# A row softmax gradient on one core: loads split by row over two queues, and some blocks stored whole

## The chip, the cores and the metric

The kernel runs on 1 core of one Trainium2 chip. The metric is device time in microseconds (us), the median of several runs. Besides the compute engines (TensorE or PE, VectorE or DVE, ScalarE or ACT, GpSimd or Pool, and SyncE or SP, which computes nothing), the core has 16 DMA engines. A DMA is issued by an instruction on one of the engines' queues (here SP, ACT or Pool); the 16 DMA engines then carry it out.

## The reference

It is the gradient of a cross-entropy loss with respect to the logits: the softmax of every row minus the one-hot label.

```python
batch, seq_len, vocab = 8, 1024, 8192       # logits float32, labels integers
logits_max = np.max(logits, axis=-1, keepdims=True)
exp_logits = np.exp(logits - logits_max)
softmax = exp_logits / np.sum(exp_logits, axis=-1, keepdims=True)
one_hot[batch_idx, seq_idx, labels] = 1.0
return (softmax - one_hot).astype(np.float32)
```

There are 8192 rows of 8192 float32 values: 268.4 MB are read and 268.4 MB are written.

## The kernel before, in words

The rows are cut into 32 blocks of 256. In a block, partition p of 128 holds rows 2p and 2p+1, which lie next to each other in memory. "Row" from here on means one such half of a block: 128 partitions times one row of 8192 values, 4 MB. There are 64 of them, numbered t = 2b + j for block b and j = 0 (even) or 1 (odd). The tile `X` has three slots (`SLOTS`) of one block each, so block b uses the slot that block b-3 used, and everything is computed in place.

For each row t the work is:

- DVE takes the row's negated maximum `m` (`row_max`), which waits for the row's load.
- ACT computes the exponential in place, with its sum `s`.
- DVE takes the reciprocal `r` of that sum.
- ACT multiplies the row by `r`.
- DVE subtracts the one-hot label: it compares `iota` (column numbers, kept in PSUM) with the label and subtracts (one `scalar_tensor_tensor`).
- ACT issues the row's store.

The order on each engine is written out by hand in the loop over t. On DVE, the maximum of row t+1 stands before the subtraction of row t. On ACT, the store of row t-1 stands between the exponential and the scaling of row t. The last row's scaling and subtraction are done in two halves.

How a block is moved is set by one letter for each block in `LOADS` and `STORES`. With `r` it goes as two transfers, one for each row: every partition moves a contiguous run of 32 KB in each. With `w` it goes as one transfer: every partition moves one run of 64 KB. (A third letter, `h`, is not used.) In `store`, a whole block goes out when its odd row is finished, since a piece is stored with the last row that it holds.

`load(b)` issues all loads on SP. Each load waits for those stores of block b-3 that meet its piece. The helper `run` (line 63) issues every instruction, gives it its waits and has it count up a semaphore. That is why nearly all lines of the profile carry L68, the line in `run` where the instruction is made. `got` are the semaphores that loads count up, `put` those of the stores, one set for each slot.

Before the change, blocks 0 to 4 and 26 to 31 are loaded by row, blocks 5 to 25 whole, and every block is stored by row.

Of the kernel before, what the change touches and what calls it, by code (L numbers as in the profile page):

```python
# [8 lines left out]
G = 2  # L9
SLOTS = 3  # L10


LOADS = "rrrrrwwwwwwwwwwwwwwwwwwwwwrrrrrr"
STORES = "rrrrrrrrrrrrrrrrrrrrrrrrrrrrrrrr"


@with_exitstack
def kernel(
# [6 lines left out]
    nc = tc.nc  # L25
# [29 lines left out]

    with tc.tile_critical():  # L56
        sem = tc.alloc_semaphore
        got = [[sem(f"got{i}{q}") for q in range(2)] for i in range(SLOTS)]
        put = [[sem(f"put{i}{q}") for q in range(2)] for i in range(SLOTS)]
        lab_got, dve, act, pe, pool = (sem(n) for n in ("lab_got", "dve", "act", "pe", "pool"))  # L60
        count = {}
# [1 line left out]
        def run(engine, waits, counter, method, **operands):  # L63

            waits = list(dict.fromkeys(waits))
            for w in waits[:-1]:
                engine.wait_ge(*w)
            instruction = getattr(engine, method)(**operands)  # L68
            for w in waits[-1:]:
                instruction._wait_ge(*w)  # L70
            step = 16 if method == "dma_start" else 1
            instruction.then_inc(counter, step)
            count[counter.name] = count.get(counter.name, 0) + step
            return counter, count[counter.name]
# [36 lines left out]
        def meets(a, b):  # L111

            sets = [[set(range(*d.indices(n))) for d, n in zip(p, (P, G))] for p in (a, b)]
            return all(x & y for x, y in zip(*sets))
# [5 lines left out]
        def load(b):  # L120
            loaded[b] = []
            before = stored.get(b - SLOTS, last_made if b == SLOTS - 1 else [])
            for q, piece in enumerate(PIECES[LOADS[b]]):
                ps, js = piece
                free = [w for other, w in before if meets(piece, other)]
                w = run(
                    nc.sync, free, got[b % SLOTS][q], "dma_start",
                    out=X[ps, b % SLOTS, js, :], in_=x_b[b, ps, js, :],
                )
                loaded[b].append((piece, w))  # L130

        def store(t):
            b, j = divmod(t, G)
            stored.setdefault(b, [])
            for q, piece in enumerate(PIECES[STORES[b]]):
                ps, js = piece
# [19 lines left out]


        load(0)
        w_max = row_max(0)
        for t in range(T):  # L160
# [7 lines left out]
            if t + 1 < T:  # L168
                if (t + 1) % G == 0:
                    load((t + 1) // G)  # L170
                w_max = row_max(t + 1)
# [53 lines left out]
```

## Time and profile before

| What | us |
|---|---|
| Median of 3 runs | 1248.09 |
| Lowest and highest run | 1247.96, 1249.02 |
| Span of the profiled execution | 1245.7 |
| DVE busy | 1119.2 |
| ACT busy | 919.1 |
| Pool busy | 7.4 |
| DVE: one row's maximum, mean | 8.68 |
| DVE: one row's subtraction, mean | 8.61 |
| ACT: one row's exponential, mean | 7.12 |
| ACT: one row's scaling, mean | 7.02 |

The span is the time from the first to the last instruction of the one execution that was profiled; no other time of that execution is on record, and the median of the timed runs is 2.4 us above its span. The page also lists, for each DMA queue, its packets, the megabytes and the time that its packets took as a share of 16 engines' span. A packet is one contiguous run that one DMA engine moves. Queue q1 is that of SP, q10 that of ACT.

### The profile page before, as it was taken

Reading aid. Unit: us, or ns where it says so; the run is one execution under the profiler, and the core shown is the slowest. Engines: PE = TensorE matmul, PEld = TensorE weight load, DVE = VectorE, ACT = ScalarE, POOL = GpSimd, SP = SyncE. Lnnn points to the kernel's source line nnn. Section 1 sums busy time; section 2 is a strip of 40 time slices with the busy share of each in tenths; the row PEclk is TensorE's granted clock in tenths of the full one; section 3 lists DMA queues with packets and bytes.
Section 4 is the critical chain, followed back from the end, with each engine's and each line's share of the span. In section 5 each row is a group of like instructions: output and inputs, shape, how many; then the busy total and the mean of one; then the engine's idle time right before and its main releaser. Section 6 shows DMA issues by size and latency. Waiting matters only on the chain.

```text
span 1245.7 us, 592 instructions
## 1 busy us (share of the span) xinstructions
PE 0.4 (0%) x2; PEld 0.3 (0%) x2; DVE 1119.2 (90%) x196; ACT 919.1 (74%) x194; POOL 7.4 (1%) x7
## 2 busy tenths in 40 slices
PE   0000000000000000000000000000000000000000
PEld 0000000000000000000000000000000000000000
DVE  5999998888988889888998888988889999999893
ACT  3888886778776787767877778777777788887772
POOL 2000000000000000000000000000000000000000
DMA  9999999999999999999999999999999999999998
GB/s 406 417 429 433 438 433 442 437 426 427 430 435 445 439 417 442 426 430 437 432 443 438 420 435 432 430 437 450 420 426 437 436 428 432 437 435 429 432 437 386
DMA packets 15460, 536.98 MB, mean 431 GB/s; under 512 B 1728, under 2 KB 1728, under 8 KB 1760
## 3 DMA queue, kind: packets, MB, share of 16 engines
q1 hardware_dynamic: 6192, 268.44, 50.0%
q10 hardware_dynamic: 9264, 268.51, 49.9%
q14 instruction: 4, 0.03, 0.0%
HBM read 268.50 MB, written 268.44 MB: 431 GB/s over the span
## 4 chain that ended last, share of the span: by engine, by line
DMA 59%; DVE 37%; another core or an unknown queue 2%; ACT 1%; DVEq 0%; issue 0%; PE 0%; SPq 0%; ACTq 0%
DMA X<-in_logits_dram 31%; DMA out_dram<-X 27%; DVE m L68 18%; DVE X L68 18%; ACT X L68 1%; DVE iota L68 0%; DVEq L56 0%; DMA lab_raw<-in_labels_dram 0%; DVE lab_f L68 0%; DVE r L68 0%; PE iota L68 0%; SPq L68 0%; ACTq L68 0%; DVE lab L68 0%
## 5 line engine op out<-in xcount | busy, mean ns | idle before, releaser
L68 DVE TENSOR_REDUCE m<-X 128x1 f32<-128x8192 f32 x64 | 555.2, 8675 | 94.3 <-DMA X<-in_logits_dram 94.3
L68 ACT ACTIVATE X<-X,m 128x8192 f32<-128x8192 f32 x64 | 455.9, 7123 | 188.4 <-DVE m L68 188.4
L68 DVE SCALAR_TENSOR_TENSOR X<-iota,lab,X 128x8192 f32<-128x8192 int16 (+1 forms) x65 | 559.7, 8612 | 4.1 <-ACT X L68 4.1
L68 ACT ACTIVATE X<-X,r 128x8192 f32<-128x8192 f32 (+1 forms) x65 | 456.0, 7017 | 115.9 <-DVE r L68 115.9
L68 DVE RECIPROCAL r<-s 128x1 f32<-128x1 f32 x64 | 9.9, 154 | 7.3 <-ACT X L68 7.3
L68 ACT ACTIVATION_READ_ACCUMULATOR X<-X,m 128x1 f32 x64 | 12.0, 187 | 0.0
L68 DVE CAST lab_f<-lab_raw 32x256 f32<-32x256 int32 x1 | 3.7, 3685 | 4.7 <-DMA lab_raw<-in_labels_dram 4.7
L68 POOL IOTA X<- 128x8192 int16 x1 | 6.9, 6944 | 0.0
L68 DVE TENSOR_SCALAR iota<-X 128x4096 int32<-128x4096 int32 x1 | 4.4, 4427 | 0.1
L68 ACT ACT_TABLE_LOAD x1 | 1.3, 1283 | 1.3 <-SPq L56 1.3
L68 DVE COPY lab<-iota 128x64 f32<-128x64 f32 x1 | 0.2, 225 | 0.5 <-PE iota L68 0.5
L68 PE MATMUL iota<-ident,lab_f 32*128 32x32 f32 x2 | 0.4, 300 | 8.5 <-DVE lab_f L68 8.5
L68 PEld LDWEIGHTS iota<-ident,lab_f 32*128 32x128 f32 x2 | 0.3, 196 | 8.4 <-DVE lab_f L68 8.4
L68 POOL TENSOR_SCALAR_AFFINE_SELECT ident<-ident 32x32 f32<-32x32 f32 x1 | 0.2, 204 | 0.1
L68 POOL MEMSET ident<- 32x32 f32 x1 | 0.1, 115 | 0.5 <-SPq L56 0.5
L209 POOL MEMSET const-bfloat16-1.0<- 128x1 bf16 x1 | 0.1, 107 | 0.0
L209 POOL MEMSET const-uint8-127<- 128x1 uint8 x1 | 0.1, 107 | 0.0
L209 POOL MEMSET const-float32-0.0<- 128x1 f32 x1 | 0.1, 104 | 0.2 <-issue 0.2
L209 POOL MEMSET const-float32-1.0<- 128x1 f32 x1 | 0.1, 104 | 0.0
## 6 DMA issues: line engine op xcount, KB each, us to landing
out_dram<-X ACTq DMA_DIRECT2D x64, 4096.0 KB, 30.8
X<-in_logits_dram SPq DMA_DIRECT2D x22, 4096.0 KB, 26.6
X<-in_logits_dram SPq DMA_DIRECT2D x21, 33.4
lab_raw<-in_labels_dram ACTq DMA_DIRECT2D x1, 64.0 KB, 3.8
```

What stands on the lines that cost most here:

```text
L68: instruction = getattr(engine, method)(**operands)
L209: nc = _bacc.Bacc("TRN2", target_bir_lowering=False, num_devices=1)
```

## The change

Three things change. All blocks are now loaded by row. From block 3 on (`SOLO`, the fourth block), the odd row of a block is issued on Pool's queue instead of SP's; even rows, and all of blocks 0 to 2, stay on SP. Blocks 6, 10, 14, 18 and 22 are stored whole, all others by row as before.

```diff
-LOADS = "rrrrrwwwwwwwwwwwwwwwwwwwwwrrrrrr"
-STORES = "rrrrrrrrrrrrrrrrrrrrrrrrrrrrrrrr"
+LOADS = "rrrrrrrrrrrrrrrrrrrrrrrrrrrrrrrr"
+SOLO = 3
+STORES = "rrrrrrwrrrwrrrwrrrwrrrwrrrrrrrrr"
...
-        got = [[sem(f"got{i}{q}") for q in range(2)] for i in range(SLOTS)]
+        got = [[sem(f"got{i}{q}") for q in range(G + 1)] for i in range(SLOTS)]
...
             for q, piece in enumerate(PIECES[LOADS[b]]):
                 ps, js = piece
                 free = [w for other, w in before if meets(piece, other)]
+                queue = nc.gpsimd if b >= SOLO and q else nc.sync
                 w = run(
-                    nc.sync, free, got[b % SLOTS][q], "dma_start",
+                    queue, free, got[b % SLOTS][G if queue is nc.gpsimd else q], "dma_start",
                     out=X[ps, b % SLOTS, js, :], in_=x_b[b, ps, js, :],
                 )
```

The loads become 64 transfers of one row, 35 on SP and 29 on Pool. The stores become 54 transfers of one row and 5 of a whole block, all on ACT. The work of DVE, ACT and PE and its order stay as they were. A load of a block whose slot was last stored whole (blocks 9, 13, 17, 21 and 25) waits, for both its rows, for that one store.

## The prediction

> **What bounds the kernel now.** I read the page first, for the engines and the DMA queues. PE and Pool are as good as unused. VectorE (DVE) is busy for 90% of the span, but the 16 DMA engines have work in 9 tenths or more of every slice but the last.
>
> ```profile
> span 1245.7 us, 592 instructions
> PE 0.4 (0%) x2; PEld 0.3 (0%) x2; DVE 1119.2 (90%) x196; ACT 919.1 (74%) x194; POOL 7.4 (1%) x7
> DMA  9999999999999999999999999999999999999998
> ...
> q1 hardware_dynamic: 6192, 268.44, 50.0%
> q10 hardware_dynamic: 9264, 268.51, 49.9%
> ...
> out_dram<-X ACTq DMA_DIRECT2D x64, 4096.0 KB, 30.8
> X<-in_logits_dram SPq DMA_DIRECT2D x22, 4096.0 KB, 26.6
> X<-in_logits_dram SPq DMA_DIRECT2D x21, 33.4
> ```
>
> Queue q1 is SP's (loads), q10 is ScalarE's (ACT, stores); together they fill 99.9% of 16 engines. That 43 loads left 6192 packets and 64 stores 9216 (plus 48 for the labels) tells how a transfer is cut: 144 packets each, which are 128 pieces, one for each partition, and 16 completions of 4 bytes. So a row transfer moves 32 KB pieces and a whole-block transfer 64 KB pieces, eight on each engine.
>
> Next come the windows, to see whether the share holds in every stage. The last two columns are the DMA share and GB/s.
>
> ```profile
> 47.00:160.00 113.00, 0.00 (x0) 0.00 (x0) 113.00 (x21) 93.66 (x20) 0.00 (x0) 1.00 1.00 428
> 160.00:940.00 780.00, 0.00 (x0) 0.00 (x0) 696.08 (x121) 575.09 (x121) 0.00 (x0) 1.00 1.00 434
> 940.00:1100.00 160.00, 0.00 (x0) 0.00 (x0) 157.03 (x28) 130.17 (x28) 0.00 (x0) 1.00 1.00 432
> 1100.00:1198.00 98.00, 0.00 (x0) 0.00 (x0) 92.38 (x17) 75.72 (x17) 0.00 (x0) 1.00 1.00 433
> 1198.00:1234.00 36.00, 0.00 (x0) 0.00 (x0) 26.29 (x5) 21.65 (x5) 0.00 (x0) 1.00 1.01 436
> ```
>
> It does: the share is 1.00 whether loads go by row (before 160 and after 940) or whole (between). The rate is 432 to 434 GB/s either way. DVE and ACT have gaps in most stages, the DMA engines none. The end is therefore set by the sum of the pieces on one DMA engine. The trace's packet records give the edges: the first data piece starts at 2.15 us, the last ends at 1244.16.
>
> Last, the timeline of the end, the only place where the order of work could still open a gap:
>
> ```profile
> 1180.42 8.69 DVE L68 TENSOR_REDUCE m<-X 128x1 f32<-128x8192 f32 x1 [1.92 <-DMA X<-in_logits_dram]
> 1197.80 0.34 ACTq L68 DMA_DIRECT2D out_dram<-X  x1
> 1199.76 8.69 DVE L68 TENSOR_REDUCE m<-X 128x1 f32<-128x8192 f32 x1 [1.93 <-DMA X<-in_logits_dram]
> 1217.14 0.34 ACTq L68 DMA_DIRECT2D out_dram<-X  x1
> 1230.18 0.34 ACTq L68 DMA_DIRECT2D out_dram<-X  x1
> ```
>
> Rows 62 and 63 reach DVE at 1180.42 and 1199.76. The last store is issued at 1230.18, 30.4 us after row 63 arrived. By the packet records the store before it keeps the engines until 1233.75. A transfer's first piece can start 1.2 us after its issue (the first load: 0.96 to 2.15), so the last issue could come until 1232.55. The end has only 2.4 us of cover.
>
> **The change, part by part.** The sum is made against the span of 1245.7; the median of the runs, 1248.09, lies 2.4 us above it, and I add the difference to that median.
>
> Pieces: every 32 KB packet record lasts 1.213 us (check on the page: 49.9% of 16 x 1245.7 us over 8192 store pieces is 1.214), every 64 KB one 2.418. Two small pieces thus cost 8 ns more than one large. Before, there are 11,008 small pieces (8192 of stores, 2816 of 22 row loads) and 2688 large ones (21 loads): (11,008 x 1.213 + 2688 x 2.418) / 16 = 1240.8 us for each engine. After, all 64 loads and 54 stores go by row, 118 x 128 = 15,104 small pieces, and five stores go whole, 640 large ones: 1241.8 us. That is +1.02. Completions rise with the transfers from 108 to 124, one of 9 ns on each engine: +0.14. Together **+1.16 us**, since nothing hides work on a resource that is full.
>
> Pool's queue: 29 loads move to it, 8 x 29 = 232 pieces on each engine, 281 us of its time. No row of before shows a load from Pool, so I bound it. Lower end of a piece: 1.213 less the 8 ns start cost, that is 1.9 us gained over 232. Upper end: the row cut into 4 KB pieces, seven more starts of 8 ns, 56 ns x 232 = 13.0 us. I take 1.213, since SP's and ACT's pieces of that size agree exactly. Pool's issue to first piece lies between 1.2 us (SP's first load) and 6.9 (Pool's longest row, the iota). I take SP's; the engines work on the queued stores meanwhile (a store lands 30.8 us after issue, while alone it needs 8 x 1.213 = 9.7).
>
> Moved waits: an odd-row load no longer stands behind the even one on SP. It waits on Pool for its own store, and nothing but later loads is queued behind it there. On SP the next even load is free to go earlier. Both queues can now be active with ACT's. That changes shares, not the sum of pieces.
>
> Whole stores: row 2b's store no longer goes out when it is done but with row 2b+1, and both loads of block b+3 wait for the whole. This must fit one turn of the three slots, 3 x 38.8 us (SP's issues at 701.98 and 740.76) = 116.3. I count, for row 2b: a load at half the engines 19.4 + 1.2 + 1.6 to its use; 34.6 from its maximum to its finished row (984.33 to 1018.89 where DVE never waits); 17.3 for the next row; the store of eight 2.418 us pieces alternating with one load queue (29.0) or two (38.8), with 1.6 for start and release. That is 104.7 to 114.5, so the fit is close but holds: 0 us. ACT's five saved issues (0.34 each) are off the path.
>
> Sum: 1248.09 + 1.16 = **1249.3**, 0.1% up. About 0.2% (2.5 us, to 1245.6 and 1250.6) is what a measurement of this kernel can tell from no change.
>
> **The rivals.** *Pool takes the engine for eight pieces at once (slower).* In the records SP and ACT alternate piece by piece: a row store lasts 17.6 us beside a row load and 10.8 alone. If Pool's row goes as one burst of 9.7 us instead, the even row on SP lands that much later. The place where it costs is row 62: it may come 2.0 us late (19.34 between the arrivals, less 17.35 of DVE work) plus the 2.4 of cover. It decides from 4.4 us on, and costs up to 9.7 - 4.4 = 5.3: 1254.6. For it speaks that no record shows Pool's queue; against, that both known queues alternate. The Trainium skill, "DMA: Bandwidth & Descriptors", section "Queues, rings and completion order", says that an engine drains a packet of typically 9 to 17 descriptors from one queue before it switches; here SP's and ACT's records contradict this, and only for Pool, with its 8 + 1, is it open.
>
> *Pool's pieces are dearer (slower).* Each per cent on them is 2.8 us; the 4 KB cut gives 1262.3. Against: the two known queues are alike. The Trainium skill, same page, section "Latency and other measured facts", calls DMA engines 7 and 15 usually slower, and ties this to descriptor rings that only GpSimd's DMAs use; no run here shows it, and it gives no size.
>
> *The whole stores starve the engines (slower).* If Pool's first piece comes at the far end, 5.7 us later, the turn above is short by up to 3.9 us at each of five stores: 1249.3 + 19.5 = 1268.8. It decides once Pool's start exceeds SP's by 1.8 us.
>
> *Pool's pieces are cheaper (faster).* Without start cost 1247.4, still no difference; to fall below 1245.6 they would have to be 3.7 us cheaper in 281, 1.3%. No row hints at that; the queue change otherwise cannot gain, as there is no idle to remove.
>
> **How the numbers follow.** Forecast 0.43 (own range 1247.4 to 1250.6); burst 0.27; dearer pieces 0.18; starved stores 0.08; cheaper 0.04. So faster 0.04, same 0.43, slower 0.53: the single likeliest case is no difference, while three kinds of harm together weigh more. The range runs from 1246.8, just under the cheapest Pool piece, to 1263, above the 4 KB cut; the starved stores' far end, the cheaper case, and worse prices than these are left out.
>
> **What would show it.** After: Pool's packets at 1.213 us, the share 1.00 in every window up to the end, the last store issued before the store ahead of it is through, and a span near 1246.9. A share under 1.00 just after the whole stores speaks for starvation, one only in the last 40 us for the burst, a share of 1.00 with a longer span for dearer pieces. A span below 1243 would make the whole reading wrong.

## The result, and the profile after

| | median of six, us | runs us | ratio to the kernel before (95%) |
|---|---|---|---|
| before | 1248.03 | 1247.41 to 1249.42 | |
| after | 1252.8 | 1248.02 to 1253.93 | 1.0032 (1.0021 to 1.0042) |

The change makes the kernel slower by 0.3%. The runs also spread over 6 us where those of before spread over 2; one run after is as short as before. The profiled execution after has a time of its own, 1253.59, and a span of 1251.8, 6.1 us more than before.

The page after, by the parts shown of before. Queue q0 is Pool's.

```profile
span 1251.8 us, 587 instructions
PE 0.4 (0%) x2; PEld 0.3 (0%) x2; DVE 1115.4 (89%) x196; ACT 919.0 (73%) x194; POOL 22.9 (2%) x36
...
q10 hardware_dynamic: 8544, 268.50, 49.7%
q1 hardware_dynamic: 5040, 146.80, 27.3%
q0 software_dynamic: 4176, 121.64, 22.7%
...
out_dram<-X ACTq DMA_DIRECT2D x54, 4096.0 KB, 41.1
X<-in_logits_dram SPq DMA_DIRECT2D x35, 4096.0 KB, 25.4
X<-in_logits_dram POOLq DMA_DIRECT2D x29, 4096.0 KB, 26.0
out_dram<-X ACTq DMA_DIRECT2D x5, 35.8
```

The cut is as forecast: 29 x 144 = 4176 packets on Pool's queue. Pool's row lands 26.0 us after its issue, SP's 25.4. The three queues still fill 99.7% of the engines, of a longer span.

The windows after show where the time goes (last two columns: DMA share and GB/s):

```profile
160.00:440.00 280.00, 0.00 (x0) 0.00 (x0) 257.86 (x45) 214.07 (x45) 3.72 (x8) 1.00 1.00 434
440.00:600.00 160.00, 0.00 (x0) 0.00 (x0) 143.06 (x26) 117.90 (x26) 2.64 (x5) 1.00 1.00 432
600.00:640.00 40.00, 0.00 (x0) 0.00 (x0) 33.96 (x7) 27.91 (x7) 0.53 (x1) 1.00 1.01 419
640.00:760.00 120.00, 0.00 (x0) 0.00 (x0) 105.75 (x19) 87.79 (x19) 1.59 (x3) 1.00 1.01 435
760.00:790.00 30.00, 0.00 (x0) 0.00 (x0) 26.27 (x6) 24.93 (x6) 0.53 (x1) 1.00 0.98 406
```

From 600 to 640 the engines have work all the time (share 1.01), and yet move 419 GB/s, not 434: the pieces themselves last longer. (In windows this short the share and the rate are rough, since a piece counts where it starts.) The packet records say it piece by piece. After 60 us, 188 pieces last over 50 ns longer than 1.213 or 2.418 us, some 32 KB pieces up to 2.47; they are called long pieces below. Together they cost 3.7 us on the average engine; before, it was 36 pieces and 0.6 us. Nearly all the lost time lies at 451 to 493, 599 to 640, 761 to 783 and 926 to 957, that is, beside and just behind the whole stores, which are issued at 433.0, 588.6, 747.6 and 903.0. Both ACT's 64 KB pieces and Pool's and SP's 32 KB pieces are long. They fall on the engines unequally: the 16 completions of one store, at most 2.4 us apart in the first 280 us, are mostly 7.6 to 12 us apart from 640 to 1180, and 16 to 17 us for the store behind each of the last three whole ones. A transfer is through only when its slowest engine is.

The end after, to set against that of before:

```profile
1205.96 8.69 DVE L69 TENSOR_REDUCE m<-X 128x1 f32<-128x8192 f32 x1 [1.15 <-DMA X<-in_logits_dram]
1223.34 0.34 ACTq L69 DMA_DIRECT2D out_dram<-X  x1
1236.37 0.34 ACTq L69 DMA_DIRECT2D out_dram<-X  x1
```

Row 63 reaches DVE at 1205.96, 6.2 us later than before, and the last store is again issued 30.4 us behind it. The records show the first piece of the store ahead starting at 1226.86 and its last piece ending at 1238.57. The engines that were early ran dry before the last store came; 1.05 us of the average engine is lost between 1232 and 1240.

### The profile page after: what moved, and what is told of

It is laid out like the page before. It is cut to its first block, busy times and chain, and to the rows that moved or that the text cites. A ratio compares the mean times of both kernels' runs of the same rounds, so it can differ in the third digit from the quotient of the medians.

```text
span 1251.8 us, 587 instructions
## 1 busy us (share of the span) xinstructions
PE 0.4 (0%) x2; PEld 0.3 (0%) x2; DVE 1115.4 (89%) x196; ACT 919.0 (73%) x194; POOL 22.9 (2%) x36
## 3 DMA queue, kind: packets, MB, share of 16 engines
q0 software_dynamic: 4176, 121.64, 22.7%
## 4 chain that ended last, share of the span: by engine, by line
DVE 60%; DMA 35%; issue 3%; ACT 1%; DVEq 0%; POOL 0%; PE 0%; ACTq 0%; SPq 0%; POOLq 0%
DVE m L69 30%; DVE X L69 29%; DMA out_dram<-X 19%; DMA X<-in_logits_dram 15%; ACT X L69 1%; DMA lab_raw<-in_labels_dram 1%; DVE iota L69 0%; DVEq L57 0%; DVE r L69 0%; DVE lab_f L69 0%; POOL X L69 0%; PE iota L69 0%; ACTq L69 0%; DVE lab L69 0%; ACTq L222 0%
## 5 line engine op out<-in xcount | busy, mean ns | idle before, releaser
L69 POOL DMA_DIRECT2D X<-in_logits_dram x29 | 15.5, 535 | 1158.6 <-DMA out_dram<-X 1158.6
L69 DVE CAST lab_f<-lab_raw 32x256 f32<-32x256 int32 x1 | 1.1, 1067 | 7.3 <-DMA lab_raw<-in_labels_dram 7.3
## 6 DMA issues: line engine op xcount, KB each, us to landing
X<-in_logits_dram SPq DMA_DIRECT2D x35, 4096.0 KB, 25.4
```

## The experiments

Theory A: pieces are stretched while whole stores run. Theory B: the end is late by itself, with or without long pieces. Rivals are named with each. All ratios are to the kernel before on the same chip.

**Again, and the parts one at a time.** The first kernel is the changed one, unaltered. The others:

```diff
# odd rows on Pool alone              # whole stores alone       # rows on one queue alone
-STORES = "rrrrrrwrrrwrrr..."         -SOLO = 3                  -SOLO = 3
+STORES = "rrrrrrrrrrrrrr..."         +SOLO = 99                 +SOLO = 99
                                                                 -STORES = "rrrrrrwrrrwrrr..."
                                                                 +STORES = "rrrrrrrrrrrrrr..."
```

Again: 

> The changed kernel once more, unaltered, for a second trace. Theory A (stretch): its pieces last longer than 1.213 and 2.418 us only while a whole store runs beside both load queues, some 2.5 us in all in the first trace, and this differs from run to run, so the six runs between 1248.0 and 1253.9 are the same mechanism met to a different degree; this trace too has its long pieces in the stretches after whole stores. Theory B (end): the last row's load always lands some 6 us late (1204.3 against 1198.2) and the end has about 1 to 3 us of idle engines; this trace shows the late landing with or without long pieces. Both: median 1251 to 1254.

Pool alone: 

> Odd rows on Pool from block 3 on, but every block stored by row. By the count of pieces: 16,384 of 1.213 us on 16 engines, +1.3, completions 128 against 108, +0.2: 1249.5. Theory A (stretch needs the 64 KB stores beside two load queues): no long pieces, share 1.00 to the end, 1249 to 1250. Rival (Pool's queue itself stretches the pieces): long pieces remain and the time is 1251 to 1254.

Whole stores alone: 

> The five whole stores as in the changed kernel, but all loads on SP. Pieces as there, +1.2. Theory A: with one load queue there is no stretch; but both loads of the block behind a whole store go one after the other on SP, so this may lose time in waits instead: 1249 to 1253, with any loss as a DMA share under 1.00 and not as long pieces. Rival (whole stores stretch pieces whatever the queues): long pieces after the five whole stores, 1251 to 1254.

Rows on one queue: 

> All loads by row on SP, all stores by row: the first of the three parts alone. Both theories: 16,384 pieces of 1.213 us and 128 completions, +1.5 us, no long pieces beyond those of the start, no idle at the end: 1249.5. A time over 1251 would show that the piece count is not what sets the time.

| kernel | median us | ratio (95%) | long pieces, us on an engine | last load's last piece at |
|---|---|---|---|---|
| again | 1252.36 | 1.0043 (1.0024 to 1.0061) | 292, 6.1 | 1210.1 |
| Pool alone | 1248.02 | 1.0001 (0.9992 to 1.0009) | 6, 0.1 | 1198.5 |
| whole stores alone | 1264.21 | 1.0121 (1.0094 to 1.0149) | 185, 5.0 | 1215.2 |
| rows on one queue | 1248.09 | 1.0002 (0.9993 to 1.001) | 4, 0.1 | 1197.5 |

The last two columns come from the packet records of the one execution profiled of each (again: one of 1258.12 us). The harm is in the whole stores; loading by row, and Pool, cost nothing that shows. Pool's pieces last 1.213 us and alternate with ACT's one by one: a row load beside row stores takes 17.9 to 18.8 us on Pool's queue, on SP's 17.9 to 18.7, where eight pieces in one burst would take 8 x 1.213 = 9.7. Here is Pool alone, the page and a window, and then the same window of the kernel before:

```profile
q0 software_dynamic: 4176, 121.64, 22.6%
...
L69 POOL DMA_DIRECT2D X<-in_logits_dram x29 | 15.4, 532 | 1153.2 <-DMA out_dram<-X 1153.2
```

```profile
160.00:1198.00 1038.00, 0.00 (x0) 0.00 (x0) 945.49 (x164) 781.33 (x165) 14.24 (x27) 1.00 1.00 433
```

```profile
160.00:1198.00 1038.00, 0.00 (x0) 0.00 (x0) 945.49 (x164) 780.99 (x164) 0.00 (x0) 1.00 1.00 433
```

Both move 433 GB/s over the 1038 us. For the whole stores on one load queue, Theory A had expected no long pieces and at most 1253; both failed. There are long pieces, nearly all in one bout, and the loads end 17 us late, which idles the end. Windows of whole stores alone:

```profile
160.00:910.00 750.00, 0.00 (x0) 0.00 (x0) 677.61 (x118) 558.78 (x118) 0.00 (x0) 1.00 1.00 434
910.00:960.00 50.00, 0.00 (x0) 0.00 (x0) 43.29 (x8) 38.18 (x9) 0.00 (x0) 1.00 0.98 387
...
1225.00:1236.00 11.00, 0.00 (x0) 0.00 (x0) 9.23 (x3) 8.63 (x3) 0.00 (x0) 1.00 0.39 167
```

The share of 0.39 near the end is the missing cover: row 63 reaches DVE at 1216.82 there, and little is left to store meanwhile. So the whole stores are cheaper with Pool's queue than without it (4.4 us against 16); why, no run here shows. "Again" speaks for Theory A: long pieces return in the same places. (By the measure used here the first trace lost 3.7 us to them, not the 2.5 of the expectation.) Theory B falls as far as the last load goes, which is not late by a fixed 6 us. That load ends at 1210.1 in "Again", 12 us late, and at 1198.6 in the kernel with three whole stores below, whose trace has next to no long pieces.

**The order of a whole store without its pieces.** Five blocks go as two row transfers, both issued when the odd row is finished. In the first kernel both loads of the block behind wait for both, in the second each for its own:

```diff
-STORES = "rrrrrrwrrrwrrr..."
+STORES = "rrrrrrdrrrdrrr..."
+            "d": [(every, slice(j, j + 1)) for j in range(G)],
-                if js.stop != j + 1:
+                if (G if STORES[b] == "d" else js.stop) != j + 1:
# only where both loads wait for both:
-                free = [w for other, w in before if meets(piece, other)]
+                free = [w for other, w in before if meets(piece, other)
+                        or (b >= SLOTS and STORES[b - SLOTS] == "d")]
```

Waiting for both: 

> The changed kernel, but the five blocks go out as two row transfers of 32 KB pieces, both issued when the odd row is finished, and both loads of the block behind wait for both: the whole store's order and waits without its 64 KB pieces. Theory A (64 KB pieces beside two load queues stretch the pieces): no long pieces after 60 us, 1248.0 to 1249.5. Rival C (the late store and the two loads let go together cost the time, whatever the pieces): long pieces remain, 1251 to 1254.

Each for its own: 

> As the kernel with late row stores, but each load of the block behind waits only for its own row's store. Theory A: 1248.0 to 1249.5, like its sister. Rival C, if the joint release of both loads is what hurts: 1248.0 to 1249.5 too while its sister is slow; if the late store alone hurts: 1250 to 1253 for both.

1248.15 us, 0.9996 (0.9987 to 1.0006), and 1248.11, 0.9999 (0.9991 to 1.0008); four and five long pieces. The first keeps every order and wait of the changed kernel and only cuts the same bytes into 32 KB pieces. (On the same chip the kernel of "The end" below, with five whole stores, measured 1.0024.) Its DVE even waits longer behind a late pair, at no cost. These are the late pair's issue, the issue of the loads behind it, and row 34 on DVE, then row 34 in the changed kernel:

```profile
589.21 0.90 ACTq L69 DMA_DIRECT2D out_dram<-X  x2
624.80 20.90 SPq L69 DMA_DIRECT2D X<-in_logits_dram  x2
657.85 8.69 DVE L69 TENSOR_REDUCE m<-X 128x1 f32<-128x8192 f32 x1 [16.67 <-DMA X<-in_logits_dram]
```

```profile
660.98 8.69 DVE L69 TENSOR_REDUCE m<-X 128x1 f32<-128x8192 f32 x1 [14.25 <-DMA X<-in_logits_dram]
```

The same two windows as above, and the end, for it:

```profile
600.00:640.00 40.00, 0.00 (x0) 0.00 (x0) 40.00 (x7) 33.75 (x8) 0.53 (x1) 1.00 1.00 433
...
760.00:790.00 30.00, 0.00 (x0) 0.00 (x0) 30.00 (x7) 24.05 (x7) 0.53 (x1) 1.00 1.01 435
```

```profile
1200.14 8.69 DVE L69 TENSOR_REDUCE m<-X 128x1 f32<-128x8192 f32 x1 [2.35 <-DMA X<-in_logits_dram]
1217.52 0.34 ACTq L69 DMA_DIRECT2D out_dram<-X  x1
1230.55 0.34 ACTq L69 DMA_DIRECT2D out_dram<-X  x1
```

433 and 435 GB/s in place of 419 and 406, and row 63 arrives at 1200.14. Rival C falls: the 64 KB store pieces do the harm, not the late store or the joint release.

**How many whole stores.** Only the letters of STORES change.

One, block 14: 

> The changed kernel with one whole store (block 14) in place of five. If each whole store costs the same, one fifth of 4.4 us: 1248.9. If the losses only build up once several have put the engines out of step (first trace: no long pieces before 450 us): 1248.0 to 1248.4. If one is enough to unsettle the rest of the run: 1250 to 1252.

Two, blocks 6 and 10: 

> The changed kernel with the first two whole stores alone (6, 10), the rest of the run by row. If losses build up with the count: 1248.0 to 1248.6. If the engines, once out of step, never come back into step: long pieces all the way to the end and 1250 or more.

Three, blocks 14, 18 and 22: 

> The changed kernel with the last three whole stores alone (14, 18, 22). In both traces nothing was lost before the second whole store, and one alone (14) cost nothing. If losses build up with the count: some 1 us, 1248.5 to 1250. If any whole store late in the run is what hurts: as five, 1251 to 1254.

| whole stores | median us | runs us | ratio (95%) |
|---|---|---|---|
| 14 | 1248.1 | 1247.78 to 1248.72 | 0.9999 (0.999 to 1.0008) |
| 6, 10 | 1248.61 | 1248.09 to 1252.95 | 1.0009 (1.0001 to 1.0018) |
| 14, 18, 22 | 1250.02 | 1247.67 to 1251.69 | 1.0014 (1.0006 to 1.0023) |
| five | 1252.8 | 1248.02 to 1253.93 | 1.0032 (1.0021 to 1.0042) |

The harm grows with the number, but by chance rather than evenly. With two, seven runs of 11 lie at 1248.09 to 1248.67 and one at 1252.95. That one was profiled, with 135 long pieces, nearly all near the two whole stores (windows):

```profile
270.00:345.00 75.00, 0.00 (x0) 0.00 (x0) 54.32 (x11) 50.72 (x12) 1.05 (x2) 1.00 1.00 423
...
430.00:500.00 70.00, 0.00 (x0) 0.00 (x0) 58.72 (x11) 53.79 (x12) 1.05 (x2) 1.00 1.00 426
500.00:1100.00 600.00, 0.00 (x0) 0.00 (x0) 550.45 (x95) 448.76 (x95) 7.92 (x15) 1.00 1.00 433
```

After 500 the rate is whole again, yet a store's completions stay 10 us or more apart until 1200, some 700 us after the last whole store landed. So the lengthening is brief, while the engines stay out of step. In the run profiled with three (1247.67, the shortest) there are 23 long pieces, 0.3 us, and next to nothing is lost. The time goes with the long pieces in the profiled runs of three, two and twice five whole stores: 0.3, 2.8, 3.7 and 6.1 us of them stand beside 1247.67, 1252.95, 1253.59 and 1258.12 us. The sentence in the expectation that nothing was lost before the second whole store does not hold in general: here the first one, block 6, lost the most.

**Equal turns, and smaller transfers.** The first kernel has the loads of before (whole in the middle, all on SP) with the five whole stores, so that load and store pieces are both 64 KB. The second stores the five blocks as two transfers of every second partition ("h" in place of "w").

Both whole: 

> The loads of the kernel before (whole from block 5 to 25, all on SP) with the five whole stores; no Pool. Load and store pieces are then of one size, 64 KB, while a whole store runs. Theory D (the harm is unequal turns: a 64 KB store piece takes twice the time of a 32 KB load piece, so loads fall behind stores): as good as no loss from that, 1248 to 1250, or a few us more if the whole loads must wait for the whole stores with nothing queued. Rival A (64 KB store pieces stretch pieces and put the engines out of step, whatever stands beside them): long pieces after the whole stores, 1251 or more.

Half the partitions: 

> The changed kernel, but the five blocks are stored as two transfers of 64 partitions each (every second partition), in 64 KB pieces; same moment, same bytes. If the size of the store's pieces does the harm: 1251 to 1254 and engines out of step, as in the changed kernel. If it is something of the one 8 MB transfer itself (a release only when all 128 pieces are through): 1248 to 1249.5.

Both whole is the slowest, 1267.83 us, 1.016 (1.0146 to 1.0174). It loses twice, and in another way than the changed kernel. Whole loads wait for whole stores with too little queued, so that the engines stand idle for some 10 us (an estimate: from 160 to 1198 the records of an engine sum to 7.8 us less than the time that passed, where in the kernel before they sum to 2.8 more). And 203 pieces are long, 10.2 us, nearly all of them loads. Windows around two of the five:

```profile
270.00:320.00 50.00, 0.00 (x0) 0.00 (x0) 48.12 (x8) 36.29 (x8) 0.00 (x0) 1.00 0.96 396
...
585.00:625.00 40.00, 0.00 (x0) 0.00 (x0) 35.52 (x7) 29.70 (x7) 0.00 (x0) 1.00 0.95 392
```

By the records these long pieces fall at two moments around each whole store: on the first piece of each engine when a load starts on idle engines (16 at 277 to 278, for one), and on the load piece that each engine has in hand when the whole store's first piece comes (15 or so each time). While a whole store's pieces pass, loads have only a fifth of the engines' time, and 1 to 5 load pieces are long. The engines stay in step: the completions of a store are at most 3.5 us apart to the end, as in kernels without whole stores (2.1 to 4.4). So this kernel does not settle Theory D. Its loss is as large as Rival A expected, but of another kind, and load and store pieces of one size hardly ran side by side. Against unequal sizes alone speaks the kernel before, with 64 KB loads beside 32 KB stores: 36 long pieces, 0.6 us.

Half the partitions: 1260.94, 1.0108 (1.0092 to 1.0123), 292 long pieces, 7.4 us in its shortest run (1255.81). Its loads and its order are those of the changed kernel. So it is the 64 KB store pieces and not the 8 MB transfer; why smaller transfers of them are worse stays open.

**The end.** The last row's store is cut into two column halves, each issued behind its half of the subtraction:

```diff
...
-        store(T - 1)
+        for q, (c, w) in enumerate(halves):
+            w = run(
+                nc.scalar, [w], put_last[q], "dma_start",
+                out=o_b[B - 1, :, G - 1, c], in_=X[:, (B - 1) % SLOTS, G - 1, c],
+            )
...
```

> The changed kernel with the last row's store cut into two column halves, the first issued 4.4 us earlier, when its half of the subtraction is done. Theory B (the end idles because the last store is issued too late; 1 to 2.3 us of the 4.4): 1250 to 1251.5, with no idle stretch before the last store. Rival (the end only follows from the long pieces): 1252 to 1252.5 as without the cut.

1251.1 us, 1.0024 (1.0013 to 1.0036), as Theory B had forecast. But the interval overlaps those of the change without the cut, 1.0032 (1.0021 to 1.0042) and 1.0043 (1.0024 to 1.0061), and the profiled execution happened to have few long pieces (45, 0.8 us), so this run does not settle what the end costs by itself.

What is shown, then: 64 KB store pieces beside 32 KB loads lengthen pieces and put the engines out of step, and the last rows come late for it. In the first trace after, against the kernel with late row stores waiting for both, the last piece ends 1250.21 - 1244.89 = 5.3 us later; long pieces make 3.7 - 0.1 = 3.6 of it. The remaining 1.7 is put down to the uneven, partly idle end, where 1.05 was read above. What lengthens a piece, why it differs from run to run, and whether it needs pieces of unequal size stays open. No kernel here beats the one before.

## Why the prediction was right or wrong

The time fell inside the range and on the slower side, to which the text gave 0.53. The forecast itself, no difference at 1249.3, did not come true, and none of the named rivals is the cause. So it was luck that the range held: its upper end was the price of Pool's row in 4 KB pieces, and the 0.53 stood for three harms of which none came as described.

- **The bound** was right. The DMA engines' work sets the time; the four kernels that changed the loads' pieces, the queues and the waits, but kept 32 KB store pieces, stayed at 1248.0 to 1248.2.
- **The count of pieces, +1.16,** is a term that was sized wrong. By the same count the kernel with only row pieces should have cost 1.5 us; it measured 1.0002 (0.9993 to 1.001), at most 1.25 us. The records overlap: from 160 to 1198 those of an engine sum to 3.4 us more than the time that passed, over 857 pieces, and in the kernel before to 2.8 us over 690. That is 4.0 ns for each piece in both. Two small pieces then cost 4 ns more than a large one and not 8, so the +1.02 for the pieces is halved (an estimate from these sums). Adding up records overstates a full engine.
- **Pool's pieces at 1.213** was right, and Pool alone is at 1.0001. In the changed kernel its first piece comes 4.1 to 5.5 us after the issue, while the other queues work, and not after the 1.2 that the prediction took; SP's comes mostly after 3.3 to 4.6. Neither shows in the time. The Trainium skill, "DMA: Bandwidth & Descriptors", section "Issuing engines are not separate DMA queues", says that issuing from several engines saves only issue time; Pool alone agrees. With the whole stores the queues did matter, 1252.36 us with Pool's and 1264.21 without.
- **The burst rival** fell. Pool's queue alternates piece by piece, so the Trainium skill's packets of 9 to 17 descriptors (same page, section "Queues, rings and completion order") are not seen on Pool's queue either.
- **Whole stores at 0 us** is the step that failed. What cost the time is the assumption under it, that a piece lasts the same whatever runs beside it: long pieces took 3.7 us in the first trace and 6.1 in the second. The trace of before held a hint: its long pieces, 36 of them, lie nearly all on the 64 KB loads, though "every" record was said to last the same.
- **The budget of one turn** under that step did not hold either. In the kernel with late row stores, waiting for both, block 14's even load is issued at 490.47 and that of block 17, in the same slot, at 624.80: 134.3 us, where 104.7 to 114.5 were counted and 116.3 were to be had. The load landed after 32.7 us (22.2 were counted to its use), the pair's stores were issued 66.1 later (51.9) and released the slot 35.6 after that (30.6 to 40.4). It cost nothing all the same, 1248.15 us, since other transfers kept the engines full (share 1.00). So the waits cost 0 us as forecast, but not for the reason given.
- **The starved stores** did not come. Pool's start lay over 1.8 us above the 1.2 of SP, the rival's own condition, and yet the share stayed at 1.00 behind the late stores, in the changed kernel from 600 to 640 and in the late-row kernel alike.
- **Dearer pieces** came true in form, a share of 1.00 with a longer span, but not for Pool's pieces as such: 102 of the 188 long ones are Pool's, yet without 64 KB stores its pieces are not dearer.
- **The cover of 2.4 us at the end** was right as a weak place: row 63 came 6.2 us late and the engines idled there.

## What to carry to other kernels

Where the DMA engines are full, do not enlarge the pieces of a transfer without a trace: larger load pieces saved nothing here, and 64 KB store pieces beside row loads cost 0.3 to 1.2%. When the share is 1.00 and the time still grows, compare GB/s by window and look for pieces that last longer than their kind. When a sum of records is to become a time, see first whether the records overlap. And when a change has several parts, run each alone first: here two of three were free and the third was hidden among them.

## What was not expected of the hardware

A 32 KB piece can take 2.47 us instead of 1.213 while 64 KB stores run beside it. The 16 DMA engines can then stay more than 10 us apart on one queue for 600 us with no later whole store. And the same program varies from 1248.02 to 1253.93 us, while of the four related kernels with 32 KB pieces alone three stay within 0.6 and one (rows on one queue) within 1.9. The kernel before, with its 64 KB loads, is not free of it: of its 32 runs on the chip of the late row stores two took 1251.21 and 1253.34 us, and no trace of those is on record.
